# A hybrid decoder layer on one core: the old sum of a block is loaded ahead, and VectorE adds a bank to it in place

## The chip, the cores and the metric

The kernel runs on one core of one Trainium2 chip. The core has five engines with a queue of instructions each: TensorE (PE; its weight loads are shown as PEld), VectorE (DVE), ScalarE (ACT), GpSimd (POOL) and SyncE (SP). Here SyncE issues nearly all DMA transfers. Matmuls write banks of PSUM; the other engines work on SBUF, and VectorE and ScalarE read PSUM too. The metric is the device time of one execution in microseconds (us), the median over runs. Smaller is better.

## The reference

One decoder layer on x of 1024 tokens by 2048 features, in fp32. A condition c gives a shift, a scale and a gate; x is normalised and modulated, projected to eight kinds of 1024 columns, used by two groups of eight heads, and projected back.

```python
mod = silu(c) @ w_ada[layer] + b_ada[layer]
shift, scale, gate = jnp.split(mod, 3, axis=-1)
h = rms_norm(x, norm_gain[layer]) * (1.0 + scale[:, None, :]) + shift[:, None, :]
proj = h @ w_in[layer]
q_sb, k_sb, v_sb, z_sb, q_r, k_r, v_r, z_r = jnp.split(proj, split_at, axis=-1)
...
oa = merge_heads(stick_breaking_attention(qa, ka, split_heads(v_sb, SB_HEADS)))
oa = oa * jax.nn.silu(z_sb.astype(jnp.float32))
...
ob = head_group_norm(chunkwise_retention(qr, kr, vr), ret_norm_gain[layer])
ob = ob * jax.nn.silu(z_r.astype(jnp.float32))
y = jnp.concatenate([oa, ob], axis=-1).astype(x.dtype) @ w_out[layer]
x = x + (gate[:, None, :] * y).astype(x.dtype)
```

For this document the two large products matter, `h @ w_in` (2048 by 8192) and the one with `w_out` (2048 by 2048). They are held transposed: 128 output features on the partitions, 1024 tokens along a row, in two halves of 512.

## The kernel before

**Groups and products.** Each large product is cut over the 2048 features that are summed into two shares of eight slices of 128. A `Group` is 256 output columns by 1024 tokens by one such share, that is a 2 by 2 block product done with seven products instead of eight (Strassen in Winograd's form). The seven are named P1, P6, P7, P2, P5, P4 and P3. A product is four steps (`j` in `range(NP)`) of three matmuls (`mm3`, L150 to L152), since both operands are split into a high and a low half. Its weights' high half is made by ScalarE (`first`, L259) and its low half by VectorE (`second`, L264), each about two products ahead in one of three buffers; sums and differences of weights (`make`, L254) are made by GpSimd.

The seven products add up in banks of PSUM, and a bank is read more than once: after P1, then again with P6 added to it, and again after P5 and P3 (`g.b`); after P7 and P4 (`g.d`); after P2 (`g.a`). So of each of the four quarters of the result (two 128-feature blocks `i` by two halves `hf`) one part comes out after P1, P6 or P7, and the other after P2, P4 or P5. The fourth quarter comes out after P3 alone.

**What is done at the end of a product.** After P1, P6 and P7, `copied` (L278 to L288) takes the bank to a tile of SBUF: a copy on ScalarE (L284, with the gate as a factor in the last product). After P2, P4 and P5, `added` (L290 to L295) has VectorE add the second bank to that tile in place, and `g.put` sends the quarter on: to memory, or through the rotary factors, a sigmoid or a square first (`second_put`), or to the final transposes (`put_y`).

**Two shares, two groups.** The groups run in one list: 16 named e (first share of `w_in`, first half of its columns; sums kept in memory as `part`), 16 named f (second share of the same columns), 16 named g (second share of the other columns, kept in `part`), 16 named h (first share of those), then 8 named y (first share of `w_out`, kept in `ypart`) and 8 named o (its second share). The groups f, h and o have a `seed`: the sum that e, g or y left in memory. For them `copied` also loads the old sum, a 128 by 512 tile (`old`, L271 to L277, a DMA on SyncE), as soon as the product has ended, and six steps later GpSimd adds it to the copy (L287). For the quarter of P3 the old sum is loaded before P4, and VectorE adds the bank to it in place (L293), without a copy.

**Tiles.** Copies come from a ring of four tiles (`pt`), old sums from a ring of three (`cp`); in the last seven groups these rings have ten and five. A ring gives the tiles out in turn: whoever writes one waits until the store of its last use has landed.

**Order of the work.** The order in which instructions enter each queue is written out by hand. A counter `now` goes up by one at the end of each step (`tick`). `at(k, fn)` runs `fn` at the k-th tick after this one; `on(k, j, fn)` runs `fn` behind step `j` of the k-th product of the whole list; the attention of the two groups of heads runs between the steps, as generators that yield the number of ticks to wait. `plan` sets the loads of weights seven and six products ahead. In the list, P4 and P3 of a group come behind P1 of the next one: P1, P4 and P3 of the group before, P6, P7, P2, P5, and so on.

Of the kernel before, what the change touches and what calls it, by code (L numbers as in the profile page):

```python
# [17 lines left out]
P = 128  # L18
# [8 lines left out]
HALF = 512  # L27
# [32 lines left out]
def layer_kernel(ctx, tc, x, c, w_ada, b_ada, norm_gain, w_in, sb_q_gain, sb_k_gain, ret_norm_gain, w_out,  # L60
# [173 lines left out]
    class Group:  # L234


        def __init__(self, w, k0, col0, name, **more):
            self.w, self.k0, self.col0, self.name = w, k0, col0, name
            self.seed, self.gate, self.put, self.done, self.pool, self.turns = None, (None, None), None, None, None, False
            self.before = None  # L240
            self.__dict__.update(more)
            self.t, self.parts, self.at, self.tell, self.early = {}, {}, {}, None, None

# [22 lines left out]

    pp = None

# [3 lines left out]
    def old(g, i, hf):  # L272

        pool, _, bufs = g.pool
        t = pool.tile([P, HALF], F32, tag="cp", bufs=bufs, name=f"cp_{g.name}_{i}_{hf}")
        nc.sync.dma_start(t, g.seed[i][:, hf * HALF:(hf + 1) * HALF])
        return t  # L277

    def copied(g, src, i, hf, name, tag="pt"):

        pool, bufs, old_bufs = g.pool
        t = pool.tile([P, HALF], F32, tag=tag, bufs=bufs if tag == "pt" else old_bufs, name=f"{name}_{g.name}")
        gt = g.gate[i]
        nc.scalar.activation(t, src, AF.Copy, scale=1.0 if gt is None else gt)  # L284
        if g.seed is not None:
            o = old(g, i, hf)
            at(6, lambda: nc.gpsimd.tensor_tensor(t, t, o, op=ALU.add))  # L287
        return t  # L288
# [9 lines left out]
    flat, events = [], {}  # L298
    ENDS = {"P2": (0, 0), "P5": (1, 1), "P4": (0, 1), "P3": (1, 0)}
    turning = [0]  # L300

# [3 lines left out]
    def plan(groups):  # L305
# [27 lines left out]
    def ended(g, p):  # L333
        if p == "P1":
            g.p1 = copied(g, g.b, 0, 0, "p1")
        elif p == "P6":
            g.u2 = copied(g, g.b, 0, 1, "u2")
        elif p == "P7":
            g.u4 = copied(g, g.d, 1, 1, "u4")
        elif p == "P3" and g.seed is None:  # L340
            g.c12 = copied(g, g.b, 1, 0, "c12", "cp")
# [15 lines left out]
    def run(ks):  # L357

        for k in ks:
# [223 lines left out]

    pp = Ring(ctx.enter_context(tc.tile_pool(name="pp", bufs=1)))
    for g in groups_a + groups_b + groups_c + groups_y:
        g.pool = (pp, 4, 3)
    staged = {}
# [216 lines left out]
    def second_put(kind, b0):  # L804
# [10 lines left out]
        def put(i, hf, t):  # L815
            dst = halves(b0 + i, hf)
            if kind in (3, 7):
# [9 lines left out]
                at(1, silu)  # L827
                store(dst, t, 6)
            elif kind in (0, 1):
# [5 lines left out]
                at(1, square)  # L835
                store(dst, t)
            elif kind in (4, 5):
# [11 lines left out]
                at(7, lambda: nc.vector.tensor_tensor(t, t, xw, op=ALU.add))  # L849
                store(dst, t, 9, lambda: free(xw))  # L850
            else:
                store(dst, t)
        return before, put
# [417 lines left out]
    new_left(groups_y, results(1))  # L1271
    groups_o[0].put, groups_o[0].pool = put_y(0), groups_y[0].pool
    until(groups_o[0], "P2")
# [4 lines left out]
    with tc.tile_pool(name="ot", bufs=1, side="right", reuse_waits="tile") as otp:  # L1278
        ot = Ring(otp)
        def finish(i):  # L1280
            xrs = []
# [6 lines left out]
            for tb in range(0, NB, 2):  # L1288
# [73 lines left out]
```

## Time and profile before

| | us |
|---|---|
| median of 3 runs | 2072.45 |
| lowest and highest run | 2071.96 and 2074.96 |
| the profiled execution | 2072.09 |
| its span, first to last instruction | 2070.3 |

The profile is of one execution. Its page lists the busy time of each engine, the share of the clock granted to TensorE over the span (0.98 in the mean), groups of equal instructions with their number, total and mean time, and the idle time in front of them with what ended it. Views of the trace give the same for a stretch of time or an engine: who waited for whom, and the instructions in order of time. In a row such as `L264 DVE TENSOR_TENSOR wl_e_P<-wr_e,wh_e_P`, L264 is the line of the kernel, DVE the engine, and the names are the tile written and the tiles read. A tile has the name of its first user: `p_e`, `u_e` and `c_e` are tiles of the two rings in all groups e to y, and `p_o`, `u_o` and `cp_o` those of the last groups.

TensorE works on the groups in these stretches: e from 104 to 469 us, f from 456 to 902, g from 892 to 1311, h from 1302 to 1707, y from 1693 to 1890, o from 1882 to 2062. The two attentions run beside f to y.

### The profile page before, as it was taken

Reading aid. Unit: us, or ns where it says so; the run is one execution under the profiler, and the core shown is the slowest. Engines: PE = TensorE matmul, PEld = TensorE weight load, DVE = VectorE, ACT = ScalarE, POOL = GpSimd, SP = SyncE. Lnnn points to the kernel's source line nnn. Section 1 sums busy time; section 2 is a strip of 40 time slices with the busy share of each in tenths; the row PEclk is TensorE's granted clock in tenths of the full one; section 3 lists DMA queues with packets and bytes.
Section 4 is the critical chain, followed back from the end, with each engine's and each line's share of the span. In section 5 each row is a group of like instructions: output and inputs, shape, how many; then the busy total and the mean of one; then the engine's idle time right before and its main releaser. Section 6 shows DMA issues by size and latency. Waiting matters only on the chain. (4 is left out here: it accounts for less than half of the span.)

```text
span 2070.3 us, 27207 instructions
## 1 busy us (share of the span) xinstructions
PE 1957.0 (95%) x9089; PEld 1564.0 (76%) x9089; DVE 1427.0 (69%) x2098; ACT 941.0 (45%) x1718; POOL 925.6 (45%) x627
## 2 busy tenths in 40 slices
PE   5879999998999999999999999899999998998998
PEld 4458777775768677788888888687788876886887
DVE  6779877566668675776766655788687887448555
ACT  4443344554455545554444444544353545345222
POOL 0434577765444235232322312677465654145443
PEclk9879999999999999999999999999999999999999
DMA  8748877533454444443433523867576877457665
GB/s 295 234 126 275 269 235 255 163 107 117 151 171 153 138 143 163 146 160 115 158 121 112 177 93 128 273 214 260 190 257 214 275 257 238 145 170 236 199 197 175
DMA packets 287329, 388.45 MB, mean 188 GB/s; under 512 B 32106, under 2 KB 164276, under 8 KB 287188
## 3 DMA queue, kind: packets, MB, share of 16 engines
q1 hardware_dynamic: 286784, 386.65, 56.9%
q8 instruction: 72, 1.18, 0.2%
q14 instruction: 69, 0.57, 0.1%
q10 hardware_dynamic: 404, 0.05, 0.0%
HBM read 278.51 MB, written 108.10 MB: 187 GB/s over the span
## 5 line engine op out<-in xcount | busy, mean ns | idle before, releaser
L264 DVE TENSOR_TENSOR wl_e_P<-wr_e,wh_e_P 128x512 fp32r<-128x512 f32 x560 | 528.9, 945 | 218.1 <-ACT wh_e_P L259 213.1
L254 POOL TENSOR_TENSOR wr_e<-wr_e,wr_e 128x512 f32<-128x512 f32 x240 | 354.6, 1492 | 495.3 <-DVE wl_e_P L264 445.7
L259 ACT ACTIVATE wh_e_P<-wr_e 128x512 fp32r<-128x512 f32 x560 | 350.7, 628 | 276.1 <-PE b_o L151 28.1
L254 POOL TENSOR_TENSOR wr_e<-wr_e 128x512 f32<-128x512 f32 x80 | 112.9, 1411 | 134.5 <-DVE wl_e_P L264 120.3
L915 DVE TENSOR_TENSOR_SCAN om<-om 128x128 f32<-128x128 f32 (+2 forms) x96 | 120.1, 1251 | 56.7 <-ACT om L906 54.9
L287 POOL TENSOR_TENSOR u_e<-u_e,c_e 128x512 f32<-128x512 f32 x50 | 79.0, 1583 | 114.9 <-DMA c_e<-part 71.8
L287 POOL TENSOR_TENSOR p_e<-p_e,c_e 128x512 f32<-128x512 f32 x49 | 74.9, 1529 | 102.2 <-DMA c_e<-part 59.4
L435 DVE SCALAR_TENSOR_TENSOR acc_b<-ada_b,silu_c,acc_b 128x512 f32<-128x512 f32 x88 | 97.3, 1106 | 27.4 <-DMA ada_b<-in_w_ada_dram 26.9
L152 PE MATMUL b_e<-S_h,wl_e_P 128*128 128x512 f32 x192 | 77.6, 404 | 7.9 <-DVE wl_e_P L264 7.7
L150 PE MATMUL b_e<-S_h,wh_e_P 128*128 128x512 f32 x192 | 77.1, 401 | 5.7 <-ACT p_e L284 5.7
L921 DVE TENSOR_TENSOR be<-be,om 128x127 f32<-128x127 f32 (+2 forms) x96 | 76.0, 792 | 7.8
L152 PE MATMUL b_h<-S_h,wl_e_P 128*128 128x512 f32 x192 | 75.7, 394 | 4.2 <-DVE wl_e_P L264 4.2
L151 PE MATMUL b_h<-S_l,wh_e_P 128*128 128x512 f32 x192 | 75.3, 392 | 3.4 <-DVE S_l L147 2.4
L962 PE MATMUL oT<-a,v 128*128 128x256 f32 x320 | 76.8, 379 | 0.0
L150 PE MATMUL b_h<-S_h,wh_e_P 128*128 128x512 f32 x192 | 76.7, 400 | 0.0
L151 PE MATMUL b_e<-S_l,wh_e_P 128*128 128x512 f32 x192 | 76.5, 398 | 0.0
L150 PE MATMUL b_f<-S_h,wh_e_P 128*128 128x512 f32 x192 | 76.3, 398 | 0.0
L150 PE MATMUL b_g<-S_h,wh_e_P 128*128 128x512 f32 x192 | 75.8, 395 | 0.0
L152 PE MATMUL b_f<-S_h,wl_e_P 128*128 128x512 f32 x192 | 74.9, 390 | 0.4 <-DVE wl_e_P L264 0.4
L151 PE MATMUL b_f<-S_l,wh_e_P 128*128 128x512 f32 x192 | 74.9, 390 | 0.0
L152 PE MATMUL b_g<-S_h,wl_e_P 128*128 128x512 f32 x192 | 74.9, 390 | 0.0
L151 PE MATMUL b_g<-S_l,wh_e_P 128*128 128x512 f32 x192 | 74.9, 390 | 0.0
(487 smaller groups left out, 5505.8 us busy)
## 6 DMA issues: line engine op xcount, KB each, us to landing
wr_e<-in_w_in_dram SPq DMA_DIRECT2D x128, 512.0 KB, 5.5
ada_b<-in_w_ada_dram SPq DMA_DIRECT2D x128, 256.0 KB, 4.7
c_e<-part SPq DMA_DIRECT2D x128, 256.0 KB, 5.2
ada_a<-in_w_ada_dram SPq DMA_DIRECT2D x64, 256.0 KB, 4.4
wr_e<-in_w_out_dram SPq DMA_DIRECT2D x32, 512.0 KB, 4.8
ld<-fin SPq DMA_DIRECT2D x54, 256.0 KB, 4.7
part<-p_e SPq DMA_DIRECT2D x48, 256.0 KB, 5.3
part<-u_e SPq DMA_DIRECT2D x48, 256.0 KB, 2.1
```

What stands on the lines that cost most here:

```text
L150: nc.tensor.matmul(o, a_hi, b_hi, start=first, stop=False, skip_group_check=True)
L151: nc.tensor.matmul(o, a_hi, b_lo, start=False, stop=False, skip_group_check=True)
L152: nc.tensor.matmul(o, a_lo, b_hi, start=False, stop=last, skip_group_check=True)
L254: nc.gpsimd.tensor_tensor(t[o], t[a], t[b], op=op)
L259: nc.scalar.activation(hi, self.t[RIGHT[p]], AF.Copy)
L264: nc.vector.tensor_tensor(lo, self.t[RIGHT[p]], self.parts[p].bitcast(F32), op=ALU.subtract)
L287: at(6, lambda: nc.gpsimd.tensor_tensor(t, t, o, op=ALU.add))
L435: nc.vector.scalar_tensor_tensor(acc, src, cj, acc, op0=ALU.mult, op1=ALU.add)
L915: nc.vector.tensor_tensor_scan(rev, rev, rev, init, op0=ALU.mult, op1=ALU.bypass)
L921: nc.vector.tensor_tensor(be[:, :m], be[:, :m], om[:, 1:m + 1], op=ALU.mult)
L962: nc.tensor.matmul(ob, v[:, j, :], a[:, cl], start=diag and ib == 0 and b == 0 and j2 == 0, stop=ch == 0 and ib == 2, skip_group_check=True)
```

## The change

For a group with a seed, the old sums of the quarters of P1, P6 and P7 are loaded one product earlier, behind the first step of the product before (`OLD`), and that of P4's load moves to the last step of the product before it. At the end of P1, P6 and P7 nothing is copied: one tick later VectorE adds the bank to the loaded tile in place (`added`), as it did for P3 alone. The ScalarE copy and the GpSimd addition of these three quarters are gone. Groups without a seed copy as before.

The rings are replaced by lists of free tiles: `sums`, seven tiles, and `more`, fifteen in the last seven groups. A tile is taken from the front of the list and is put back at its end when its store has been issued (or, in the last groups, when its last transposes are written down).

```diff
     def old(g, i, hf):

-        pool, _, bufs = g.pool
-        t = pool.tile([P, HALF], F32, tag="cp", bufs=bufs, name=f"cp_{g.name}_{i}_{hf}")
+        t = g.old[i, hf] = g.pool.pop(0)
         nc.sync.dma_start(t, g.seed[i][:, hf * HALF:(hf + 1) * HALF])
-        return t
-
-    def copied(g, src, i, hf, name, tag="pt"):
-
-        pool, bufs, old_bufs = g.pool
-        t = pool.tile([P, HALF], F32, tag=tag, bufs=bufs if tag == "pt" else old_bufs, name=f"{name}_{g.name}")
+
+    def copied(g, src, i, hf):
+
         gt = g.gate[i]
+        if g.seed is not None:
+            t = g.old.pop((i, hf))
+            at(1, lambda: added(g, t, src, i))
+            return t
+        t = g.pool.pop(0)
         nc.scalar.activation(t, src, AF.Copy, scale=1.0 if gt is None else gt)
-        if g.seed is not None:
-            o = old(g, i, hf)
-            at(6, lambda: nc.gpsimd.tensor_tensor(t, t, o, op=ALU.add))
         return t
...
+    OLD = {"P1": (0, 0, 0), "P6": (0, 1, 0), "P7": (1, 1, 0), "P4": (1, 0, 3)}
...
+            if p in OLD:
+                on(k - 1, OLD[p][2], lambda g=g, p=p: g.seed is not None and old(g, *OLD[p][:2]))
...
             if p == "P3":
                 if g.seed is not None:
+                    g.c12 = g.old.pop((1, 0))
                     added(g, g.c12, g.b, 1)
...
-            elif p == "P4" and g.seed is not None:
-                g.c12 = old(g, 1, 0)
...
-            store(dst[b0 + i][:, hf * HALF:(hf + 1) * HALF], t, 4)
+            store(dst[b0 + i][:, hf * HALF:(hf + 1) * HALF], t, 4, lambda: sums.append(t))
...
+    sums.extend(pp.tile([P, HALF], F32, tag=f"pt{i}", bufs=1, name=f"pt{i}") for i in range(7))
     for g in groups_a + groups_b + groups_c + groups_y:
-        g.pool = (pp, 4, 3)
+        g.pool = sums
...
+        more = [otp.tile([P, HALF], F32, tag=f"pt{i}", bufs=1, name=f"ot{i}") for i in range(15)]
...
+                if tb % 4 == 2 and i:
+                    more.extend(quarters[i, e, tb // 4] for e in range(2))
...
-                g.put, g.pool = put_y(i), (ot, 10, 5)
+                g.put, g.pool = put_y(i), more
```

The stores of `second_put` put their tiles back into `sums` in the same way.

More of the change, by code (lines that the diff above doesn't have):

```diff
@@ L241, in __init__ @@
             self.__dict__.update(more)
-            self.t, self.parts, self.at, self.tell, self.early = {}, {}, {}, None, None
+            self.t, self.parts, self.at, self.old, self.tell, self.early = {}, {}, {}, {}, None, None
         def load(self, i):
@@ L265, in second @@
             self.parts[p] = self.parts[p], lo
-    pp = None
+    sums = []
     def bank(i, name):
@@ L334, in ended @@
         if p == "P1":
-            g.p1 = copied(g, g.b, 0, 0, "p1")
+            g.p1 = copied(g, g.b, 0, 0)
         elif p == "P6":
-            g.u2 = copied(g, g.b, 0, 1, "u2")
+            g.u2 = copied(g, g.b, 0, 1)
         elif p == "P7":
-            g.u4 = copied(g, g.d, 1, 1, "u4")
+            g.u4 = copied(g, g.d, 1, 1)
         elif p == "P3" and g.seed is None:
-            g.c12 = copied(g, g.b, 1, 0, "c12", "cp")
+            g.c12 = copied(g, g.b, 1, 0)
         def add():
@@ L581, in layer_kernel @@
     stp.__exit__(None, None, None)
-    pp = Ring(ctx.enter_context(tc.tile_pool(name="pp", bufs=1)))
+    pp = ctx.enter_context(tc.tile_pool(name="pp", bufs=1))
+    sums.extend(pp.tile([P, HALF], F32, tag=f"pt{i}", bufs=1, name=f"pt{i}") for i in range(7))
     for g in groups_a + groups_b + groups_c + groups_y:
-        g.pool = (pp, 4, 3)
+        g.pool = sums
     staged = {}
@@ L827, in put @@
                 at(1, silu)
-                store(dst, t, 6)
+                store(dst, t, 6, lambda: sums.append(t))
             elif kind in (0, 1):
@@ L835, in put @@
                 at(1, square)
-                store(dst, t)
+                store(dst, t, 2, lambda: sums.append(t))
             elif kind in (4, 5):
@@ L849, in put @@
                 at(7, lambda: nc.vector.tensor_tensor(t, t, xw, op=ALU.add))
-                store(dst, t, 9, lambda: free(xw))
+                store(dst, t, 9, lambda: (free(xw), sums.append(t)))
             else:
-                store(dst, t)
+                store(dst, t, 2, lambda: sums.append(t))
         return before, put
@@ L1271, in layer_kernel @@
     new_left(groups_y, results(1))
-    groups_o[0].put, groups_o[0].pool = put_y(0), groups_y[0].pool
+    groups_o[0].put, groups_o[0].pool = put_y(0), sums
     until(groups_o[0], "P2")
```

## The prediction

> **What bounds the kernel now.** I read the page's busy table first, then busy time by stage, then who waits for whom on TensorE, then the instructions by order of time around the largest waits.
>
> ```profile
> span 2070.3 us, 27207 instructions
> PE 1957.0 (95%) x9089; PEld 1564.0 (76%) x9089; DVE 1427.0 (69%) x2098; ACT 941.0 (45%) x1718; POOL 925.6 (45%) x627
> 456.00:902.00 446.00, 428.99 (x1864) 322.99 (x1863) 305.89 (x459) 222.86 (x413) 189.25 (x127) 0.98 0.46 148
> 1302.00:1707.00 405.00, 384.13 (x1879) 315.22 (x1879) 326.25 (x494) 190.29 (x341) 256.60 (x166) 0.99 0.72 242
> 1890.00:2062.00 172.00, 165.34 (x771) 135.75 (x770) 101.80 (x122) 54.05 (x89) 79.98 (x58) 0.98 0.60 197
> ```
>
> TensorE is busy 95% of the span; 113 us are left. The last three rows are the only stages in which anything is changed: the groups named f (456 to 902 us), h (1302 to 1707) and o (1890 to 2062), which start from an old sum in memory. The columns are the stretch and its length, then busy time of PE, weight loads, DVE, ACT and POOL, then clock and DMA. There TensorE idles 17.0, 20.9 and 6.7 us, 44.6 us together: no edit in these stages can win much more. DVE is busy 69%, 81% and 59% of them.
>
> ```profile
> PE b_f L152 <- DVE wl_e_P L264: 7.0, 2, 6.6
> PE zp L900 <- DVE k L884: 6.5, 3, 3.2
> PE b_h L152 <- DVE wl_e_P L264: 8.9, 8, 2.0
> PE otp L1162 <- ACT v L755: 4.1, 3, 1.4
> PE d_o L152 <- DVE wl_e_P L264: 6.0, 1, 6.0
> ```
>
> These are the long rows of TensorE's waits in f (two), h (two) and o (one): total, number, longest. Nearly all are for VectorE, which is late with the low half of the weights (L264) or of k (L884). No row of these stages waits for a copy (L284), the instruction that goes. So the change acts on the bound only by what it does to VectorE, and to ScalarE and GpSimd in front of it.
>
> ```profile
> L264 DVE TENSOR_TENSOR wl_e_P<-wr_e,wh_e_P 128x512 fp32r<-128x512 f32 x560 | 528.9, 945 | 218.1 <-ACT wh_e_P L259 213.1 <-PE zp L899 3.8
> ...
> L287 POOL TENSOR_TENSOR u_e<-u_e,c_e 128x512 f32<-128x512 f32 x50 | 79.0, 1583 | 114.9 <-DMA c_e<-part 71.8 <-ACT u_e L284 19.2 <-ACT om L906 17.0
> ...
> L287 POOL TENSOR_TENSOR p_e<-p_e,c_e 128x512 f32<-128x512 f32 x49 | 74.9, 1529 | 102.2 <-DMA c_e<-part 59.4 <-ACT p_e L284 31.3 <-ACT A_h L146 4.6
> 764.56 1.71 POOL L287 TENSOR_TENSOR u_e<-u_e,c_e 128x512 f32<-128x512 f32 x1
> 765.08 1.74 DVE L884 TENSOR_TENSOR k<-ld,k 128x512 fp32r<-128x512 f32 x1
> 766.74 0.68 DVE L884 TENSOR_TENSOR q<-ld,q 128x512 fp32r<-128x512 f32 x1
> ...
> 766.87 0.58 PE L900 MATMUL zp<-k,q 128*128 128x256 f32 x1 [3.15 <-DVE k L884]
> ```
>
> Here is why VectorE is late. The same subtraction takes 1.74 us while a GpSimd addition runs and 0.68 us right after it: 1.06 us lost. The mean of L264, 945 ns, is such a mixture. The GpSimd addition in this picture, L287, is one of those that the change takes away.
>
> **The change, part by part.** Sums are made against the profiled execution: 2072.1 us, of which the span is 2070.3 and 1.8 lie around it; the median of the runs is 2072.45, 0.4 more.
>
> Removed: in 40 groups (16 f, 16 h, 8 o) three ScalarE copies and three GpSimd additions each, 120 of both. Added: 120 VectorE additions of a bank to a loaded tile.
>
> ```profile
> L284 ACT ACTIVATE p_e<-b_f x16: 597/598/602, 459.1 to 851.0; 128x512 f32<-128x512 f32 x16
> L284 ACT ACTIVATE u_o<-b_o,gate_c x6: 691/691/691, 1921.8 to 2039.1; 128x512 f32<-128x512 f32 x6
> L293 DVE TENSOR_TENSOR c_e<-b_f,c_e x16: 678/691/692, 500.8 to 902.0; 128x512 f32<-128x512 f32 x16
> L295 DVE SCALAR_TENSOR_TENSOR cp_o<-b_o,gate_c,cp_o x7: 749/751/752, 1940.0 to 2062.8; 128x512 f32<-128x512 f32 x7
> ```
>
> The numbers behind the count are shortest, median and longest in ns. ScalarE loses 96 x 0.60 + 24 x 0.69 = 74 us. GpSimd loses 99 at some 1.56 us and 21 more, about 185 us. VectorE gains 96 x 0.69 + 24 x 0.75 = 84 us; L293 and L295 are just the instruction that is added, in the same stages, and they keep 0.68 to 0.75 us whatever GpSimd does (shortest and longest lie 14 ns apart).
>
> What VectorE gets back: an L287 costs it 1.06 us when it falls on a subtraction and nothing when VectorE is idle. By the busy shares, 48 x 0.69 + 48 x 0.81 + 24 x 0.59 = 86 of the 120 meet a busy VectorE, at most 86 x 1.06 = 91 us. So VectorE's work stays about the same, 84 more and up to 91 less. I take it as even. Bounds: 84 us more work if GpSimd's other operations slide onto the same subtractions, 91 less if the additions all fall into idle time.
>
> The Trainium skill speaks against the direction: "Perfetto Trace Analysis", Optimizing Scalar/DVE Operations, says that a saturated VectorE may be helped by moving work from it to ScalarE or even GpSimd, and the change does the reverse. It also gives VectorE a larger overhead on a bank (about 125 ns) than on SBUF (about 60). The trace doesn't show the second: 0.68 to 0.69 us both for L293, which reads a bank, and for an unhindered L884, which doesn't; with 65 ns more each, an estimate, the 120 would cost 8 us more.
>
> Where it meets the path, place by place. In f, three waits for k (6.5 us in the row above): one L287 beside each, 1.06 back, and the new addition of the same product stands 0.69 in front: 0.4 each, 1.2 us. At the start of f and of o, and in the heads of h:
>
> ```profile
> 479.51 3.42 POOL L287 TENSOR_TENSOR u_e<-u_e,c_e 128x512 f32<-128x512 f32 x2
> ...
> 1899.98 3.46 POOL L287 TENSOR_TENSOR u_e<-u_e,c_e 128x512 f32<-128x512 f32 x2
> ...
> 1905.60 5.08 DVE L147 TENSOR_TENSOR S_l<-ld,S_h 128x512 fp32r<-128x512 f32 x3
> ...
> 1908.43 1.71 POOL L287 TENSOR_TENSOR p_o<-p_o,cp_o 128x512 f32<-128x512 f32 x1
> ...
> 1911.34 0.79 PE L152 MATMUL d_o<-A_h,wl_e_P 128*128 128x512 f32 x1 [5.97 <-DVE wl_e_P L264]
> 1464.18 0.50 PE L152 MATMUL b_h<-A_h,wl_e_P 128*128 128x512 f32 x1 [1.98 <-DVE wl_e_P L264]
> ...
> 1560.13 3.14 POOL L287 TENSOR_TENSOR p_e<-p_e,c_e 128x512 f32<-128x512 f32 x2
> ...
> 1562.13 1.16 DVE L141 TENSOR_TENSOR u<-y 128x8 f32<-128x8 f32 x1
> ...
> 1563.72 0.17 DVE L141 TENSOR_TENSOR u<-y 128x8 f32<-128x8 f32 x1
> ...
> 1565.78 0.50 PE L152 MATMUL b_h<-A_h,wl_e_P 128*128 128x512 f32 x1 [1.32 <-DVE wl_e_P L264]
> ...
> 1667.17 0.50 PE L152 MATMUL b_h<-A_h,wl_e_P 128*128 128x512 f32 x1 [1.04 <-DVE wl_e_P L264]
> ```
>
> Before the 6.6 us wait of f stand two L287: 2 x (1.06 - 0.69), 0.8 us. Before the 5.97 us wait of o stand three, 5.2 us, while VectorE's splits take 1.7 us each: 3 x 1.06 back, 3 x 0.72 added, 1.0 us. In h, a retention head's small chain stops behind an L287 (the 8-element L141 takes 1.16 us instead of 0.17), and TensorE then waits 1.32 us; 1.98 and 1.04 us at two other heads. There 1.0 to 1.1 comes back and 0.69 is added: 0.4 each, 1.2 us. Where no L287 is near a wait, one addition stands in front without anything back:
>
> ```profile
> 1408.68 0.60 ACT L284 ACTIVATE u_e<-d_h 128x512 f32<-128x512 f32 x1 [2.14 <-DMA fin<-u_e]
> ...
> 1409.85 0.50 PE L152 MATMUL b_h<-S_h,wl_e_P 128*128 128x512 f32 x1 [1.52 <-DVE wl_e_P L264]
> ```
>
> That is +0.7 us. But the same rows show a wait that goes: the ScalarE copy stood 2.14 us until its ring buffer's store had landed, and the high halves of the weights are queued behind it. A list of seven tiles replaces the rings. By the due times in the code a tile is held for 30 (P1 and P6), 18 and 11 steps of a group's 28, with the rotary factors 7 more each: 89/28 = 3.2 to 117/28 = 4.2 of the seven are in use, and the next one is long free. I give 0.7 us for that. Sum of the places: 1.2 + 0.8 + 1.0 + 1.2 - 0.7 + 0.7 = 4.2 us.
>
> A wait can also cost twice:
>
> ```profile
> 1465.90:1469.30 3.40, 3.24 (x10) 2.75 (x11) 2.23 (x4) 2.02 (x6) 0.00 (x0) 0.50 0.94 301
> ```
>
> After the wait at 1464 us the clock granted (the 0.50) is half for 3.4 us, which costs 1.7 us. I count half of one such stretch as saved, 0.9 us: 5.1 us in all.
>
> Hidden at no cost: ScalarE's 74 us lie beside TensorE already. Their effect is that the high half L259, for which L264 waited 213.1 us in its row, can start when the product ends; VectorE's new addition (0.69) runs beside it (0.63 us). If VectorE is already behind, this cover is gone and the addition costs its 0.69.
>
> The wait added: VectorE now waits for the seed's load, and behind it on VectorE stand the weights' low halves, for which TensorE waits two products later (between P1 and P6, P6 and P5; P7 and P4 are further apart).
>
> ```profile
> 1311.26 0.39 PE L150 MATMUL b_h<-S_h,wh_e_P 128*128 128x512 f32 x1
> ...
> 1311.94 0.39 PE L150 MATMUL b_h<-S_h,wh_e_P 128*128 128x512 f32 x1
> 501.89 0.38 SPq L276 DMA_DIRECT2D c_e<-part  x1
> ...
> 504.64 0.60 ACT L284 ACTIVATE p_e<-b_f 128x512 f32<-128x512 f32 x1 [0.90 <-PE b_f L152]
> DMA to landing us min/median/max: 2.6/5.3/7.8
> ```
>
> Three matmuls take 0.68 us, so the seven steps from the new place (one step into the product before) to the product's end take 4.8 us, more where attention lies between. SyncE runs ahead of its place: this load was issued 2.7 us before the end of the product behind which it is written. 4.8 + 2.7 = 7.5 us stand against a landing of 5.3 (last row, of L276). P4's load, in the kernel before, has one step more, and VectorE shows no wait for it. So I count nothing; a wait of up to 7.8 - 4.8 = 3 us is the other bound, hidden by the two products (5.4 us) unless VectorE is behind. Past SyncE's queue, the three loads go up by seven steps each; the stores that they pass wait for results anyway.
>
> **The rivals.**
> 1. *VectorE becomes the bound in h* (slower). It is at 81% there. If the remaining GpSimd work (L254, L845) slides onto the subtractions that L287 leaves, nothing comes back, and each of the 14 waits for L264 and L884 in the rows above gets its 0.7 us: 9.8, plus one more half-clock stretch, 1.7: about 2083. It decides once VectorE is over 85% busy in h. For: the 81%, and the wait of 1409.85. Against: 48 x 1.56 = 75 of GpSimd's 257 us in h are L287. The skill's rule on a saturated VectorE, quoted above, would lead here.
> 2. *The places by L287 close altogether*: the waits for k (6.5), three heads (4.3, and 4.1 of the otp row), half of both stage starts (6.3) are 21 us, without the clock; taken at 15, as not all will: 2057. The Trainium skill's "SBUF — State Buffer", Who interferes with whom, has the loser of the port that VectorE and GpSimd share stand for the whole other instruction; by that each L287 returns its 1.5 us, not 1.06. In the row of 765.08 it is 1.06, as the addition had run for 0.5 us.
> 3. *Nothing reaches TensorE*: gains and additions cancel, 2072.
> 4. *The free list does not help*: if a popped tile's store has not landed, SyncE stands and loads come late; with about four of seven in use I give it no share of its own; its price, some waits of 2 us (as at 1408.68), lies within rival 1.
>
> **How the numbers follow.** Forecast 2072.1 - 5.1 = 2067, its own range 2063 to 2070, chance 0.40. Rival 1: 0.18. Rival 2: 0.20. Rival 3: 0.22. A measurement of this kernel tells about 0.2% from no change, 4.1 us, so faster begins under 2068.3. Three quarters of the forecast's 0.40 and all of rival 2 lie there: 0.50. Same: 0.22 and the rest, 0.32. Slower: 0.18. The range, 2054 to 2084, reaches to rivals 1 and 2 and leaves out their tails.
>
> **What would show it.** L284 and L287 gone from f, h and o; L264's mean in h under its present value, L884 at 0.68; TensorE's waits for k under 6 us. Against me: VectorE rows that wait for c_e loads by more than 1 us, which would move the low halves; TensorE's waits for L264 in h above 8.9 us, which is rival 1; k's waits gone and o's start under 3 us, which is rival 2.

## The result and the profile after

| | us |
|---|---|
| before, median of 4 runs beside it | 2073.7 (2071.96 to 2075.61) |
| after, median of 4 runs | 2044.95 (2041.57 to 2046.85) |
| ratio, with its 95% interval | 0.9853 (0.9835 to 0.987) |
| the profiled execution of after, its span | 2045.0, 2043.1 |

The forecast was 2067.0, the range 2054 to 2084. The kernel became faster as forecast, but by 28.8 us (2073.7 - 2044.95) instead of 5.1, and it lies below the range. Two rows of the page of after, the span and the busy time of the engines:

```profile
span 2043.1 us, 26981 instructions
PE 1949.2 (95%) x9089; PEld 1561.3 (76%) x9089; DVE 1414.5 (69%) x2218; ACT 882.9 (43%) x1598; POOL 737.3 (36%) x507
```

VectorE (DVE) has 120 instructions more and 12.5 us less busy time than before (1427.0); ScalarE lost 58 us, GpSimd 188. To see where the time went, the stages f, h and o are cut at the same matmuls in both kernels (the counts of matmuls agree to one). First before, then after; the columns are those of the prediction's first fence.

```profile
456.00:892.00 436.00, 418.99 (x1813) 314.65 (x1812) 297.60 (x444) 215.55 (x398) 188.72 (x126) 0.98 0.46 148
1302.00:1693.00 391.00, 372.10 (x1813) 305.42 (x1813) 314.81 (x475) 183.77 (x329) 249.19 (x161) 0.99 0.72 243
1882.00:2070.30 188.30, 176.05 (x824) 144.42 (x822) 112.84 (x138) 59.59 (x99) 82.00 (x60) 0.98 0.61 199
```

```profile
462.00:887.00 425.00, 415.06 (x1812) 312.60 (x1812) 287.21 (x495) 193.83 (x350) 114.10 (x78) 0.99 0.48 152
1297.00:1673.00 376.00, 365.32 (x1813) 301.65 (x1812) 311.11 (x523) 161.84 (x283) 172.14 (x114) 1.00 0.76 252
1860.00:2043.10 183.10, 174.59 (x823) 143.80 (x821) 115.92 (x162) 45.68 (x75) 47.21 (x35) 0.99 0.65 203
```

f is 11.0 us shorter, h 15.0, o 5.2: 31.2 us in all (of the rest, y is 2.0 us shorter, g alike, and the stretch from 104 us to the cut before f 6.0 longer, with ten more matmuls in it). Two things make the 31.2. TensorE's idle time, length less busy time, fell from 17.0 to 9.9, from 18.9 to 10.7 and from 12.3 to 8.5: 19.0 us. And the same matmuls took less time: 3.9, 6.8 and 1.5 us less busy, 12.2 in all, at a higher granted clock. The waits of TensorE behind the first part (view of the waits, after; total, number, longest):

```profile
PE b_f L152 <- DVE wl_e_P L264: 4.2, 1, 4.2
PE zp L902 <- DVE k L886: 3.7, 6, 2.4
PE d_o L152 <- DVE wl_e_P L264: 3.0, 1, 3.0
...
PE vtp_vT L756 <- DMA vT<-fin: 2.4, 3, 1.9
...
PE otp L1164 <- ACT v L757: 1.5, 3, 0.7
...
PE b_h L152 <- DVE wl_e_P L264: 0.7, 2, 0.4
```

The row of b_h fell from 8.9 to 0.7: the waits at the three heads of h, 4.3 of it, are gone, and so is that at 1409 us, 1.5 (another 1.7, at 1704 us, lies beyond the cut, in y). The others are about halved (7.0 to 4.2, 6.0 to 3.0, 4.1 to 1.5). In f the three waits for k fell from 6.5 to 3.1 (2.04, 3.15 and 1.26 to 0.48, 2.41 and 0.19), the rest of this row lies elsewhere. One wait is longer: 1.9 us for a load of v (vT, 1412 us), 0.6 before. Behind the second part stand the stretches at half clock. Windows of 3.4 us, the first of twice that, before and then after, at three places (the last number but two is the granted clock):

```profile
766.20:773.00 6.80, 6.13 (x15) 4.89 (x16) 4.07 (x6) 1.63 (x4) 1.99 (x3) 0.50 0.25 77
1465.90:1469.30 3.40, 3.24 (x10) 2.75 (x11) 2.23 (x4) 2.02 (x6) 0.00 (x0) 0.50 0.94 301
1568.30:1571.70 3.40, 3.40 (x12) 2.72 (x11) 1.46 (x3) 1.23 (x4) 0.00 (x0) 0.50 1.01 313
```

```profile
766.00:769.40 3.40, 2.58 (x12) 2.21 (x13) 3.21 (x8) 1.15 (x3) 0.00 (x0) 1.00 0.13 37
1454.00:1457.40 3.40, 3.01 (x17) 2.58 (x18) 2.88 (x5) 2.25 (x6) 0.00 (x0) 1.00 0.98 302
1551.70:1555.10 3.40, 3.40 (x19) 2.91 (x20) 2.88 (x6) 2.21 (x6) 0.00 (x0) 1.00 0.92 287
```

At the two heads of h (1465 and 1568 us before) the waits for the low halves are gone, and the clock is no longer halved behind them. At the wait for k (766 us) TensorE still waits 2.41 us instead of 3.15, and the clock stays full all the same; so a wait alone does not decide it, and what does is not shown here. Counted in pieces of 3.4 us, the trace of before has ten at half clock in f, h and o (five, three, two; at 486, 766 and 1909 us two follow one another), that of after four (three, none, one): six fewer, 6 x 1.7 = 10.2 of the 12.2 us. The other 2.0 are not resolved here. In y it is the other way round: one piece before, three after, from 1690.9 to 1701.1 us. These counts are of one execution each.

What VectorE does, grouped (after: total us, mean ns of one, idle time in front of it and what ended that):

```profile
L264 DVE TENSOR_TENSOR wl_e_P<-wr_e,wh_e_P 128x512 fp32r<-128x512 f32 x560 | 494.7, 884 | 119.4 <-ACT wh_e_P L259 119.2
...
L292 DVE TENSOR_TENSOR pt<-b_f,pt 128x512 f32<-128x512 f32 x64 | 43.9, 687 | 69.3 <-PE b_f L152 69.2
...
L292 DVE TENSOR_TENSOR pt<-b_h,pt 128x512 f32<-128x512 f32 x64 | 43.7, 683 | 6.9 <-PE b_h L152 6.9
```

The additions from the bank keep 0.68 to 0.69 us, as forecast. The low halves of the weights fell from 945 to 884 ns each, and from 213 to 119 us of waiting for the high half. The start of f shows the exchange; VectorE in order of time, before and then after:

```profile
474.30 2.38 DVE L147 TENSOR_TENSOR S_l<-ada_b,S_h 128x512 fp32r<-128x512 f32 x2
476.61 1.78 DVE L264 TENSOR_TENSOR wl_e_P<-wr_e,wh_e_P 128x512 fp32r<-128x512 f32 x1
478.31 5.16 DVE L147 TENSOR_TENSOR A_l<-xT,A_h 128x512 fp32r<-128x512 f32 x3
483.40 4.01 DVE L147 TENSOR_TENSOR S_l<-xT,S_h 128x512 fp32r<-128x512 f32 x3
487.34 0.68 DVE L264 TENSOR_TENSOR wl_e_P<-wr_e,wh_e_P 128x512 fp32r<-128x512 f32 x1
```

```profile
479.06 0.68 DVE L147 TENSOR_TENSOR S_l<-ada_b,S_h 128x512 fp32r<-128x512 f32 x1
479.67 0.68 DVE L292 TENSOR_TENSOR pt<-b_f,pt 128x512 f32<-128x512 f32 x1
480.27 1.19 DVE L147 TENSOR_TENSOR S_l<-ada_b,S_h 128x512 fp32r<-128x512 f32 x1
481.38 1.78 DVE L264 TENSOR_TENSOR wl_e_P<-wr_e,wh_e_P 128x512 fp32r<-128x512 f32 x1
483.09 0.68 DVE L292 TENSOR_TENSOR pt<-d_f,pt 128x512 f32<-128x512 f32 x1
483.69 4.61 DVE L147 TENSOR_TENSOR A_l<-xT,A_h 128x512 fp32r<-128x512 f32 x3
488.22 1.88 DVE L147 TENSOR_TENSOR S_l<-xT,S_h 128x512 fp32r<-128x512 f32 x3
490.03 0.68 DVE L264 TENSOR_TENSOR wl_e_P<-wr_e,wh_e_P 128x512 fp32r<-128x512 f32 x1
```

From the first of these splits to the last low half's start it was 13.0 us before (474.30 to 487.34) and is 11.0 after (479.06 to 490.03), with two additions more in it. The three splits that still take 4.61 us stand beside GpSimd's other work: sums of weights (L254) and splits (L147) run there from 479.29 to 487.75 us without a gap.

### The profile page after: what moved, and what is told of

It is laid out like the page before. It is cut to its first block, busy times and chain, and to the rows that moved or that the text cites. A ratio compares the mean times of both kernels' runs of the same rounds, so it can differ in the third digit from the quotient of the medians.

```text
span 2043.1 us, 26981 instructions
## 1 busy us (share of the span) xinstructions
PE 1949.2 (95%) x9089; PEld 1561.3 (76%) x9089; DVE 1414.5 (69%) x2218; ACT 882.9 (43%) x1598; POOL 737.3 (36%) x507
## 5 line engine op out<-in xcount | busy, mean ns | idle before, releaser
L254 POOL TENSOR_TENSOR wr_e<-wr_e,wr_e 128x512 f32<-128x512 f32 x240 | 351.0, 1476 | 746.4 <-DVE wl_e_P L264 679.2
L264 DVE TENSOR_TENSOR wl_e_P<-wr_e,wh_e_P 128x512 fp32r<-128x512 f32 x560 | 494.7, 884 | 119.4 <-ACT wh_e_P L259 119.2
L254 POOL TENSOR_TENSOR wr_e<-wr_e 128x512 f32<-128x512 f32 x80 | 109.4, 1367 | 256.1 <-DVE wl_e_P L264 236.5
L917 DVE TENSOR_TENSOR_SCAN om<-om 128x128 f32<-128x128 f32 (+2 forms) x96 | 111.6, 1163 | 43.7 <-ACT om L908 41.4
L292 DVE TENSOR_TENSOR pt<-b_f,pt 128x512 f32<-128x512 f32 x64 | 43.9, 687 | 69.3 <-PE b_f L152 69.2
L908 ACT ACTIVATE om<-zp,rq 128x128 f32<-128x128 f32 (+2 forms) x96 | 56.0, 584 | 61.6 <-PE zp L903 54.0
L923 DVE TENSOR_TENSOR be<-be,om 128x127 f32<-128x127 f32 (+2 forms) x96 | 69.9, 728 | 8.0 <-DVE om L917 0.5
```

The costliest lines, as they stand in the source:

```text
L254: nc.gpsimd.tensor_tensor(t[o], t[a], t[b], op=op)
L264: nc.vector.tensor_tensor(lo, self.t[RIGHT[p]], self.parts[p].bitcast(F32), op=ALU.subtract)
L292: nc.vector.tensor_tensor(t, src, t, op=ALU.add)
L908: nc.scalar.activation(om[:, :n], zp[:, :n], AF.Sigmoid, scale=rq[:, h, 1, i:i + 1])
L917: nc.vector.tensor_tensor_scan(rev, rev, rev, init, op0=ALU.mult, op1=ALU.bypass)
L923: nc.vector.tensor_tensor(be[:, :m], be[:, :m], om[:, 1:m + 1], op=ALU.mult)
```

## The experiments

Each kernel ran beside the kernel before on the same chip. The table gives the median, the ratio to before with its interval, and the gain, the median of before in the same call less this median. Before was 2073.3 to 2076.2 in these calls, so gains of different calls are good to some 2 or 3 us. Busy time is that of VectorE in the profiled execution.

| run | median us | ratio (95%) | gain us | VectorE busy us |
|---|---|---|---|---|
| the change | 2044.95 | 0.9853 (0.9835 to 0.987) | 28.8 | 1414.5 |
| gpsimd_back | 2066.57 | 0.9961 (0.995 to 0.9973) | 8.6 | 1455.2 |
| scalare_back | 2047.86 | 0.9882 (0.9859 to 0.9905) | 27.3 | 1411.7 |
| both_back | 2069.52 | 0.9981 (0.9966 to 0.9995) | 5.6 | 1464.5 |
| vector_for_gpsimd | 2058.03 | 0.9932 (0.9912 to 0.9952) | 17.1 | 1431.7 |
| list_and_ahead | 2074.05 | 0.9994 (0.9983 to 1.0006) | -0.1 | 1436.7 |
| ahead_vector | 2058.93 | 0.9925 (0.9901 to 0.9948) | 15.0 | 1422.6 |
| late_load | 2054.06 | 0.9899 (0.9874 to 0.9924) | 19.9 | 1410.3 |
| vector_twice | 2058.75 | 0.9921 (0.9894 to 0.9947) | 15.2 | 1474.4 |
| ahead_at_6 | 2046.52 | 0.9852 (0.9819 to 0.9884) | 27.6 | 1404.3 |
| no_gpsimd_add | 2038.1 | 0.9814 (0.9786 to 0.9841) | 36.0 | 1341.6 |
| more_to_vector | 2032.74 | 0.9791 (0.9764 to 0.9818) | 41.3 | 1408.8 |
| most_to_vector | 2030.39 | 0.978 (0.9755 to 0.9806) | 43.7 | 1419.3 |
| queue_only | 2083.53 | 1.0043 (1.0024 to 1.0063) | -7.4 | 1401.2 |
| queue_short | 2043.75 | 0.9846 (0.9823 to 0.9869) | 29.6 | 1415.4 |
| vector_twice_sbuf | 2072.21 | 0.9985 (0.997 to 1.0001) | 3.9 | 1493.5 |
| half_weights | 2010.54 | 0.9687 (0.9663 to 0.9712) | 65.6 | 1442.1 |
| all_weights | 2006.47 | 0.9667 (0.9644 to 0.9689) | 69.7 | 1467.5 |
| all_left | 2000.54 | 0.9636 (0.961 to 0.9662) | 72.8 | 1465.6 |

### Which engine's work it was

Theory: the gain is GpSimd's, since its additions hold up VectorE's subtractions. Rivals: ScalarE's copies stood before the high halves; the list and the early loads. Three kernels put the removed work back into the changed one, on a scratch tile (taken from the list, which then has six):

```diff
+            nc.scalar.activation(spares[0], src, AF.Copy, scale=1.0 if gt is None else gt)          # scalare_back, both_back
             at(1, lambda: added(g, t, src, i))
+            s = spares[0]
+            at(6, lambda: nc.gpsimd.tensor_tensor(s, s, s, op=ALU.add))       # gpsimd_back, both_back
```

> The changed kernel with 120 GpSimd additions put back, on a tile that nothing else uses, six steps after P1, P6 and P7 as before (the list is six tiles instead of seven to make room). Theory G (the gain is that GpSimd no longer holds up VectorE's two-input operations): 20 us or more come back, 2063 to 2075 us. Theory S (the gain is ScalarE's copies gone from in front of the weights' high halves) and theory L (the gain is the tile list and the earlier loads): under 2051 us.

> The changed kernel with 120 ScalarE copies of the bank put back at the end of P1, P6 and P7, into a tile that nothing reads (list of six tiles). Theory S: 15 us or more come back, 2060 to 2073 us. Theories G and L: under 2051 us.

> The changed kernel with both put back, the ScalarE copies and the GpSimd additions on the copy's tile; VectorE's additions, the loads ahead and the list (six tiles) stay. Theories G and S together: 2070 to 2085 us, at or over the kernel before, since VectorE's additions are on top. Theory L: under 2055 us.

GpSimd's additions take back 20.2 us of the gain (28.8 - 8.6), ScalarE's copies 1.5, both 23.2. The copies' part is no more than runs differ. The busy times on the page of gpsimd_back:

```profile
PE 1955.6 (95%) x9089; PEld 1564.1 (76%) x9089; DVE 1455.2 (70%) x2219; ACT 882.0 (43%) x1598; POOL 894.8 (43%) x627
```

and its group of additions put back, among the groups by line:

```profile
L285 POOL TENSOR_TENSOR scr<-scr 128x512 f32<-128x512 f32 x120 | 158.9, 1324 | 2.9
```

VectorE has the work of after and one memset, and is busy 41 us longer (1455.2 for 1414.5). In scalare_back the low halves' wait for the high half stayed at 122 us with the copies back (VectorE's additions wait 114 us for the copies there, and the time hardly moves); in ahead_at_6, below, which has no copies but adds later, it is 188. So its fall from 213 is for the larger part a matter of the turn and not of the copies.

The other side, one line of the kernel before (L287 on VectorE, with ScalarE's copies, rings and late loads as they were):

```diff
-            at(6, lambda: nc.gpsimd.tensor_tensor(t, t, o, op=ALU.add))
+            at(6, lambda: nc.vector.tensor_tensor(t, t, o, op=ALU.add))
```

> The kernel before with one thing changed: the 120 additions of copy and old sum run on VectorE instead of GpSimd, at the same place; ScalarE's copies, the late loads and the rings stay. Theory G: most of the gain is there, 2045 to 2055 us. Theory S: 2065 to 2076 us. Theory L: 2070 to 2078 us.

17.1 us come from that word alone, more than half of the change's gain. At 2058.0 it lies 3 us above theory G's range; the next runs look for the rest.

### Lists, early loads, the bank, the turn

Four kernels stand between before and after. The step from ahead_vector to ahead_at_6 takes away the copy and the second SBUF operand together.

```diff
# list_and_ahead: the lists and the loads ahead; ScalarE copies, GpSimd adds at turn 6
         t = g.pool.pop(0)
         nc.scalar.activation(t, src, AF.Copy, scale=1.0 if gt is None else gt)
+        if g.seed is not None:
+            o, pool = g.old.pop((i, hf)), g.pool
+
+            def plus():
+                nc.gpsimd.tensor_tensor(t, t, o, op=ALU.add)     # ahead_vector: nc.vector
+                pool.append(o)
+            at(6, plus)
# ahead_at_6: no copy, the bank added in place, but
-            at(1, lambda: added(g, t, src, i))
+            at(6, lambda: added(g, t, src, i))
# late_load: as ahead_at_6, and the old sum is loaded only when the product has ended
```

> The list of seven tiles and the loads one product ahead, with ScalarE's copies and GpSimd's additions kept as in the kernel before (the old sum's tile goes back to the list when GpSimd's addition is written down). Theory L (lists and loads give the 5 to 9 us that are left when GpSimd's and ScalarE's work is put back): 2065 to 2070 us. Theory G alone, without L: 2072 to 2078 us.

> As the run before, but the addition of copy and old sum is VectorE's instead of GpSimd's, six steps after the product, both inputs in SBUF; ScalarE's copies stay. It differs from the run that only moved the additions to VectorE (2058 us) by the list and the loads ahead. Theory G+L (VectorE there stood behind late loads): 2045 to 2051 us, as the run with ScalarE's copies put back. If the rest of the gain came from adding the bank in place: 2055 to 2060 us.

> The changed kernel with the loads of P1, P6 and P7 back at the product's end and VectorE's addition of the bank six steps later. Theory G+L: VectorE waits for late loads and TensorE for the low halves: 2053 to 2065 us. If the loads' lead is worth nothing (as predicted: no wait counted): 2043 to 2048 us.

> The changed kernel with the loads ahead as they are, but with VectorE's addition from the bank asked for at turn 6 instead of turn 1. Theory 'source': what the bank brings over an addition of two tiles in SBUF is its duration alone (0.68 us beside a busy GpSimd, against 0.84), so the turn does not matter: 2045 to 2049 us. Theory 'turn': the addition is free because at turn 1 it falls where VectorE waits for ScalarE's next high half; at turn 6 it stands before work that TensorE waits for, as in the run with the SBUF addition on VectorE (2058.9): 2053 to 2059 us, and VectorE's wait for the high halves goes back up from 119 us.

Gains, step by step: the lists and early loads -0.1; VectorE for GpSimd 15.0; the bank added directly instead of a copy of it 27.6; turn 1 for turn 6 28.8. So 15.1 + 12.6 + 1.2 us. list_and_ahead and ahead_vector take two tiles of the list for a quarter where the change takes one, and their copies wait for stores (24 us in all in ahead_vector, 5 in after); so the -0.1 does not price the list as the change uses it. The theory "turn" fell: at turn 6 the wait for the high halves went up to 188.5 us and the time by 1.2, which is within what calls differ, so that wait was slack. The early load does matter for the bank addition: late_load is 7.7 us worse than ahead_at_6, and VectorE then shows the wait that after doesn't have (wait view of late_load):

```profile
DVE pt L293 <- DMA pt<-part: 19.7, 9, 4.3
```

Of the 12.6 us for the bank, 1.5 is the copy by scalare_back. For the rest there are two candidates: those waits for stores, and the source of the addition. The source is tested by a second, idle addition in the changed kernel, from the bank or from SBUF alone:

```diff
             at(1, lambda: added(g, t, src, i))
+            s = spares[0]
+            at(1, lambda: nc.vector.tensor_tensor(s, src, s, op=ALU.add))     # vector_twice
+            at(1, lambda: nc.vector.tensor_tensor(s, s, s, op=ALU.add))       # vector_twice_sbuf
```

> The changed kernel with a second VectorE addition of the bank, into a tile that nothing reads, beside each of the 120 (list of six tiles): 83 us more on VectorE. By the prediction's sum VectorE's additions cost 0.7 us at each place where TensorE waits, some 10 to 15 places: 2052 to 2058 us. If they run in VectorE's idle time: under 2050 us. If VectorE is the bound in h: over 2060 us.

> As the run with a second bank addition on VectorE (13.8 us over the changed kernel), but the second addition is of two operands in SBUF, on a scratch tile. Theory 'source' (an addition of SBUF tiles is held up beside GpSimd, and holds GpSimd up; one from the bank is not): 8 to 12 us more than that run, 2066 to 2071 us, and the added instruction's mean well over 0.69 us. Rival: the source does not matter, 2056 to 2061 us.

The second set costs 13.6 us from the bank and 24.9 from SBUF. One group of vector_twice, then the group of vector_twice_sbuf:

```profile
L285 DVE TENSOR_TENSOR scr<-b_f,scr 128x512 f32<-128x512 f32 x32 | 21.7, 679 | 0.0
```

```profile
L285 DVE TENSOR_TENSOR scr<-scr 128x512 f32<-128x512 f32 x120 | 99.2, 826 | 0.0
```

With both operands in SBUF the mean is 826 ns, from the bank 679: 147 ns x 120 = 18 us more work for 11 us more time, about what the step to the bank gained, so little is left for the waits for stores. Both times lie about 1 us above the range of their theory (2058.75 over 2058, 2072.2 over 2071). The Trainium skill's "SBUF — State Buffer", Who interferes with whom, says that a VectorE instruction with two SBUF inputs contends with a GpSimd instruction that reads SBUF, and one with a single SBUF input does not; these means, and L292's unmoved 0.68, agree.

no_gpsimd_add takes L287 out of the kernel before and puts nothing in its place:

> The kernel before without GpSimd's 120 additions: the copies and the loads of the old sums stay, three quarters of the outputs of seeded groups lack the first half of the features. If GpSimd's additions cost what giving them back cost (21.6 us), and the additions on VectorE cost what a second set of them cost (13.8), then without either: 2073.5 less 16 less 14, 2040 to 2048 us. If moving them to VectorE (2058) had taken away all that they cost, VectorE doing them for nothing: 2056 to 2060 us.

It gains 36.0 us, and VectorE, with the same 2098 instructions as before, is busy 85.4 us less (1341.6 for 1427.0). So 120 GpSimd additions held VectorE up 0.71 us each in the mean and cost 36 us in this kernel. 120 bank additions on VectorE in their place cost 7 (36.0 - 28.8; some 9 if the copies, which this run keeps, cost 1.5), though VectorE is busy 73 us more with them (1414.5 for 1341.6).

### Through VectorE, or through GpSimd's own queue?

Both would make GpSimd's additions dear: they could also delay its sums of weights (L254), for which the high halves wait. Tiny additions fill the same queue:

```diff
             at(1, lambda: added(g, t, src, i))
+            s = spares[0][:, 0:8]
+            at(6, lambda: [nc.gpsimd.tensor_tensor(s, s, s, op=ALU.add) for _ in range(12)])   # queue_short: range(5)
```

> The changed kernel with six tiles in the list, and for each of the 120 bank additions twelve additions of 8 elements a partition on GpSimd at turn 6, on a scratch tile: they hold GpSimd's queue for about as long as one large addition did (1.3 us in the run that gave 120 of them back), and touch little. Theory 'queue' (the weights' combinations come late): the 21.6 us come back, 2062 to 2067 us. Theory 'VectorE held up beside GpSimd': 2044 to 2050 us.

> As queue_only with five tiny additions on GpSimd in place of twelve: by the 288 ns that one took there, 1.44 us for each bank addition and 173 us in all, beside 1.32 and 159 us of the large additions of gpsimd_back (2066.6, 21.6 us over the changed kernel). Theory 'queue': 2062 to 2068 us. Theory 'VectorE held up beside GpSimd': 2045 to 2051 us, and ScalarE's waits for GpSimd's combinations near the 23 us of the changed kernel. Between the two, 2052 to 2061: both.

queue_only was over-dosed: the 1440 tiny additions held GpSimd for 415 us, 2.6 times the 159 of gpsimd_back, and ScalarE's high halves then waited 88 us for L254 (23 in after). Held that long, the queue costs 36 us by itself. queue_short has the right dose; its busy times:

```profile
PE 1945.5 (95%) x9089; PEld 1557.2 (76%) x9089; DVE 1415.4 (69%) x2219; ACT 881.7 (43%) x1598; POOL 915.1 (45%) x1107
```

and its group of tiny additions:

```profile
L285 POOL TENSOR_TENSOR scr<-scr 128x8 f32<-128x8 f32 x600 | 185.9, 310 | 40.4
```

GpSimd is as busy as in gpsimd_back (915.1 and 894.8 us), VectorE as in after (1415.4 and 1414.5), and the time is that of after (gain 29.6). The two runs differ in what the additions do to VectorE, 40 us of its busy time, and by 21.0 us of gain. ScalarE even waits longer for GpSimd in queue_short (35 us for L254 and 20 for the tiny additions) than in gpsimd_back (29 and 6) or in after (23), and nothing is lost by it. This settles it for a queue held that long: the cost goes through VectorE. Part of it is the clock: the trace of gpsimd_back has ten pieces of 3.4 us at half clock in f, h and o, as before, that of queue_short three and a part of one. It also shows that a list of six tiles does as well as seven.

### How far it goes

If a GpSimd operation costs more than the same one on VectorE, the others should be moved too: rotary products, the additions into `acc_b` and `kp` (more_to_vector, 88), the sums of the left operand read back (most_to_vector), two and then all four of the weights' combinations (half_weights, all_weights), and every fourth split (all_left). Each edit has this form:

```diff
-            nc.gpsimd.tensor_tensor(t[o], t[a], t[b], op=op)
+            nc.vector.tensor_tensor(t[o], t[a], t[b], op=op)
```

> The changed kernel with 88 more of GpSimd's operations on VectorE: the rotary multiplications (32), the additions into acc_b (28) and those of kp (28). Theory 'GpSimd costs wherever it works beside VectorE': 0.13 us for each, as in the run that moved the 120 additions (16 of 120), so some 11 us: 2031 to 2038 us. Rival 'only at the ends of products': the 120 additions stood where TensorE's next operand was due, these stand on a schedule of their own, many in stages where TensorE is 99% busy (g: 409.4 of 410): 2043 to 2048 us, or slower by what VectorE's own work costs (0.115 each, 10 us: 2055).

> The same with the four kinds of operation that combine the tiles of the left operand read back (27, in e) and every fourth split that went to GpSimd also on VectorE, some 140 operations in all moved; GpSimd keeps the weights' combinations (L254) alone. Theory 'GpSimd costs wherever it works beside VectorE': 0.13 us each, 18 us: 2025 to 2032 us. Rival: no better than the run with 88, or worse by 0.115 us for each of the 52 more, 6 us.

> As the run with some 140 operations moved to VectorE (2030.4), and two of the four weight combinations of a block (L254, 160 of 320) too. By the same rule of 0.13 us for each operation moved: 2008 to 2015 us. Rival: VectorE's own work now costs as much as GpSimd's did, since VectorE waits less and is due more often: 2026 to 2034 us. If VectorE becomes the bound of f and h: over 2035.

> As before it, with all 320 combinations of the weights on VectorE. GpSimd's 460 us go, VectorE's own rise by 220 less what it is no longer held up: in h VectorE was busy 311 of 376 us and gets 64 of these, 44 us, and loses up to 9 to 13 for each hundred: 345 of 370. By the rule of 0.13 us: 1988 to 1995 us, which would be under TensorE's own 1940 and its gaps of 90, so 2000 to 2015 at best. Rival, VectorE as the bound of h and f: 2035 to 2070 us.

> As all_weights (2006.5) with every fourth split of the left operand, which GpSimd did, on VectorE too (some 24 operations of 1.7 us). By 0.13 us for each: 2003 us. Rival: in h and o the splits of a block now stand one behind another on VectorE at a stage's start, where TensorE waits for them: 2006 to 2012 us.

most_to_vector moved 32 operations more than more_to_vector, 120 in all; the splits stayed, against its description. The gains over the change are 12.5, 14.9, 36.8, 40.9 and 44.0 us. Up to half_weights that is 0.12 to 0.14 us for each operation moved (280 there); the last 160 weight combinations brought only 4.1, and the 28 splits 3.1. The rivals that had VectorE as the bound fell. all_left is the best version, ratio 0.9636. Its busy times:

```profile
PE 1929.8 (97%) x9089; PEld 1558.1 (78%) x9089; DVE 1465.6 (73%) x2686; ACT 884.7 (44%) x1598; POOL 49.0 (2%) x39
```

The low halves of the weights in all_left, by line:

```profile
L264 DVE TENSOR_TENSOR wl_e_P<-wr_e,wh_e_P 128x512 fp32r<-128x512 f32 x560 | 387.3, 692 | 84.2 <-ACT wh_e_P L259 83.4 <-issue 0.2
```

And VectorE in order of time at the start of f in all_left (in brackets the idle time before, and for whom it waited):

```profile
453.83 2.49 DVE L147 TENSOR_TENSOR A_l<-xT,A_h 128x512 fp32r<-128x512 f32 x4
456.24 2.49 DVE L147 TENSOR_TENSOR S_l<-xT,S_h 128x512 fp32r<-128x512 f32 x4
458.64 0.68 DVE L264 TENSOR_TENSOR wl_e_P<-wr_e,wh_e_P 128x512 fp32r<-128x512 f32 x1
...
464.83 0.69 DVE L292 TENSOR_TENSOR pt<-b_f,pt 128x512 f32<-128x512 f32 x1 [2.50 <-PE b_f L152]
```

VectorE does 468 operations more than after and is busy 51 us longer, and a low half takes 692 ns instead of 884. At the start of f eight splits take 0.6 us each, where six took 1.3 to 1.7 before; TensorE waits 1.95 us for the low half there instead of 6.6, and from 464.83 us on it is VectorE that waits for the end of TensorE's products.

## Why the prediction was right or wrong

**What bounds the kernel: right.** TensorE's waits for VectorE were what the change shortened. The bound of 44.6 us on idle time held, but it was no bound on the gain: 12.2 of the 31.2 us in f, h and o are matmuls that run faster, outside idle time.

**VectorE's work "as even": right as a sum, wrong as a conclusion.** Busy time changed by -12.5 us; GpSimd's additions gave back 85 us (no_gpsimd_add) of the at most 91, and the additions brought 73 of the 84. (The "91 less" was no bound of the sum: 84 are added in any case, so its best is 7 less.) The weighing of the two is the step that failed. The prediction set a microsecond that comes back against a microsecond that is added (1.06 back, 0.69 in front, 0.4 for a place), as if both had the same price for TensorE. The runs give two prices. The time that GpSimd's additions hold VectorE up: 41 us for 20.2 (gpsimd_back), 85 us for 36.0 (no_gpsimd_add). A bank addition: 7 us for the 120 (no_gpsimd_add against after), 13.6 for 120 more (vector_twice). Why it is so cheap is only argued: L292 shows 69 us of waiting for the end of f's products, so VectorE has slack there; ahead_at_6, as fast at another turn, says that this place is not the only one with slack.

**The places: 4.2 us forecast, 19.0 measured.** The waits for k in f gave 3.4 instead of 1.2, the three heads of h 4.3 instead of 1.2, the start of f and o 2.8 and 3.0 instead of 0.8 and 1.0; the otp row gave 2.6 where nothing was counted, and the wait at 1409 us, which was to grow by 0.7, lost its 1.5. The subtraction of 0.69 at each place was most of the error: at the start of f two additions were in front, as forecast, and the low half came 2.1 us sooner, not 0.8. At a wait for k the forecast shows its picture (after, in order of time):

```profile
764.08 1.48 DVE L923 TENSOR_TENSOR be<-be,om 128x512 f32<-128x512 f32 x1
...
765.49 0.68 DVE L292 TENSOR_TENSOR pt<-b_f,pt 128x512 f32<-128x512 f32 x1
766.09 0.67 DVE L886 TENSOR_TENSOR k<-ld,k 128x512 fp32r<-128x512 f32 x1
...
766.82 0.39 PE L902 MATMUL zp<-k,q 128*128 128x256 f32 x1 [2.41 <-DVE k L886]
```

k's subtraction takes 0.67 instead of 1.74 with an addition in front of it, and the wait is 2.41 instead of 3.15: 0.74, near the 0.4 forecast. Here it held; at the other two waits for k in f it did not.

**The clock: 0.9 us forecast, 12.2 measured in f, h and o.** Half of one piece of 3.4 us was counted; six of ten went, 10.2 us.

**ScalarE hidden: right.** 74 us of copies are worth about 1.5. **The wait for the seed: right.** No instruction that adds a seed waits for its load in after by the wait view. **The list and the ring wait: 0.7 forecast, not priced.** list_and_ahead gained nothing, but it uses the list for two tiles a quarter. In after no addition waits for a store, and the wait at 1409 us is gone, so of the two terms there, 0.7 less and 0.7 more, the second at least was wrong. Near its place TensorE now waits 1.9 us for the load of v.

**The rivals.** Rival 1 (VectorE bounds h) fell: VectorE is at 83% of h (311.11 of 376) and its waits shrank; all_left, with far more work on VectorE, is faster still. Rival 2 had the mechanism, and by its marks after lies between it and the forecast (o's start 3.0, k not gone); the places gave 19.0 of its 21 us, of which it took 15, and it left out the clock. The 1.5 us that each L287 was to return by the rule cited there (the section speaks of the whole instruction for VectorE's two-port modes) is too much: it is 0.71 in the mean (no_gpsimd_add), nearer to the forecast's 1.06 for those that meet a busy VectorE. Rivals 3 and 4 fell. The Trainium skill's offer to relieve a saturated VectorE through GpSimd, weighed in the prediction, does not hold here, with VectorE at 69%; the section itself adds that moving work between these two might not help. The same page ("Perfetto Trace Analysis", Optimizing GPSIMD Operations) prefers other engines to GpSimd where possible, and every run of the last series agrees.

**What stays open.** 2.0 us of the faster matmuls, and which waits bring a piece at half clock; why a bank addition costs so little; how much of the 36.8 us of half_weights is VectorE held up less and how much is weights that are ready sooner, since L254 itself became shorter (1476 to 776 ns); whether a turn between 1 and 6 beats both.

## What to carry to other kernels

Don't weigh VectorE's work as one sum of busy time: time in which GpSimd holds up instructions that TensorE is due to read cost here 0.4 to 0.5 us per microsecond, while additions from a bank cost 0.1 to 0.2. Where GpSimd works on large SBUF tiles beside a VectorE that feeds TensorE, try the operation on VectorE, and let it read a bank rather than a copy of it. When waits of TensorE close, count the pieces at half clock behind them as well: here six of ten went.

## What the runs showed of the hardware

- VectorE's addition of 128 by 512 took 678 to 689 ns in the mean with one operand in a bank, whatever GpSimd did, and 826 to 912 ns in the mean of the large groups with both operands in SBUF beside a working GpSimd (vector_twice_sbuf, ahead_vector, vector_for_gpsimd).
- Five or twelve GpSimd additions of 8 elements a partition took 288 to 310 ns each and left VectorE's busy time as it was (1415.4 and 1401.2 us); one of 512 elements took 1324 ns and added 41 us / 120 = 0.34 us to VectorE's in the mean.
- GpSimd's addition of a tile to itself took 1324 ns, of two tiles (L287) 1529 to 1583 in the two largest groups and 1329 and 1461 in those of o.
- The granted clock fell to 0.50 for 3.4 us or a multiple of it, 1.7 us lost in each piece: behind a wait of 3.15 us for k (before, 766 us), but not behind one of 2.41 at the same place (after).
